# Forgetting attention: scores of two heads as 64-row products on the two halves of the array, for two query blocks in a row

## The chip, the cores and the metric

The kernel runs on one core of a Trainium2 chip. The time is the device time of one execution in microseconds; the figure for a kernel is the median of its runs. One further execution is recorded by the hardware profiler, and the rows shown in this document come from it. In the rows, PE is the matrix engine (TensorE) with its 128 x 128 array, PEld its weight loads, DVE the vector engine, ACT the scalar engine, POOL the GpSimd engine and SP the engine that mostly issues DMAs.

## The reference

A decoder of two layers over 512 positions of width 1024, in fp32. Layer 0 is a dilated windowed attention with a gated convolution network, layer 1 a forgetting attention with the same kind of network. The change lies in layer 1's attention. It has 16 heads of width 64; keys and values are made once from the residual stream, and so is a forget gate per head, whose cumulated logarithm `c` is added to the scores:

```python
for i in range(T // BLK):                      # blocks of 128 queries
    q0, q1 = i * BLK, (i + 1) * BLK
    s = einsum('bqhd,bkhd->bhqk', q[:, q0:q1], k[:, :q1]) * scale
    s = s + (c_t[:, :, q0:q1, None] - c_t[:, :, None, :q1])
    p = softmax(where(causal, s, NEG))
    outs.append(einsum('bhqk,bkhd->bqhd', p, v[:, :q1]))
```

Query block i sees the keys 0 to 128(i+1) - 1, so its scores are 128 by 128(i+1) for each head.

## The kernel before

**Number format.** Most products are made from fp32 values split in two parts, a high part rounded to the fast format fp32r and a low part, the remainder. A product then needs three terms: high times high, high times low, low times high (`mm3`, lines 263 to 266). Transposes and the product of probabilities and values are plain fp32.

**Work per head pair and unit.** Heads go in pairs, j = 0 to 7; head `2j + hh` has the 64 features `64hh` to `64hh + 63` of a 128-row chunk. A unit is (j, i), one pair and one query block, 32 in all, in order of j and then i. Scores are computed with the queries as weights (128 queries) and the keys as the moving operand, over `nn = max(128(i+1), 256)` columns.

**Stacked operands.** With heads of 64 features a score product would use only 64 of the array's 128 rows. The kernel stacks the two parts of an operand over the rows. For a key head, `keys` (line 1392) puts the high part in the 64 rows where the projection left it and the low part in the other 64 rows. For queries, `q_high` and `q_low` (lines 1505 and 1514) do the same for version 0 of a tile; two DMAs of 256 KB each, line 1523 and line 1524, copy it with its row halves exchanged into version 1. One product of 128 rows with version 0 then gives high times high plus low times low, and one with version 1 gives high times low plus low times high: `f_scores` (line 1583) makes two products per head, four per unit. For i < 2 the scores of both heads share a PSUM bank, for i >= 2 each head has a bank of its own. The DMAs are issued by SP, those of pair 0 by POOL.

**Order.** Every engine takes its instructions in the order in which the program writes them. The loop over n (line 1672) writes, for unit n: its scores (PE); the normalisation of unit n-1 (`f_norm`, DVE); the softmax of unit n (`f_exp`: on DVE, line 1604, the scaled score plus bias and its running extreme, on ACT, line 1606, the exponential with its sum); the bias of unit n+1 (`f_bias`, POOL); at i = 1 the low part of the next pair's queries; a quarter of a query projection for a later pair, six products of 512 columns (`q_part`, PE); the transposes of unit n-2's probabilities (`f_transpose`, PE, and ACT's copy at line 1630); and at i = 2 the products with the values for the four units of the pair before (`f_pv`, PE), whose 64-column halves serve one head each. At i = 0 follows the cast of the next pair's queries (`q_high`, ACT). In between, the weights for the output projection are loaded by SP (line 49), cast by ACT (line 57) and split by DVE (line 69). When no queries are left to project, from the seventh pair on, products of the output projection (`po`, tile `acc`) take their place.

**Buffers.** The eight PSUM banks are one pool; a new tile takes the bank that was released first in program order. Keys, queries, weights and outputs of the attention come from a pool of 16 tiles of 8 KB per partition (`t8`), biases, probabilities and raw weights from one of 10 tiles of 4 KB (`t4`).

Layer 0 has a related score product (lines 1111 and 1113): plain fp32, 64 rows, two heads on the two halves of the rows, not stacked. The profile shows each of its fp32 products as two passes.

Of the kernel before, what the change touches and what calls it, by code (L numbers as in the profile page):

```python
# [9 lines left out]
F32 = mybir.dt.float32  # L10
F32R = mybir.dt.float32r
BF16 = mybir.dt.bfloat16
AF = mybir.ActivationFunctionType
ALU = mybir.AluOpType

D = 1024
T = 512
# [86 lines left out]
def trunk_kernel(ctx, tc, x, norm_gains, w_qkv_a, w_o_a, w_q_b, w_o_b, kv_norm, w_kvf, b_f,  # L104
                 w_up, conv_w, conv_b, w_down, rope, out):
    nc = tc.nc
    act, dve, pool, pe, sp = nc.scalar, nc.vector, nc.gpsimd, nc.tensor, nc.sync
# [8 lines left out]
    def t8(shape, dt=F32, name="t8"):  # L116
        return p8.tile(shape, dt, tag="t8", name=name)

    def t4(shape, dt=F32, name="t4"):
        return p4.tile(shape, dt, tag="t4", name=name)  # L120
# [4 lines left out]
    def bank(shape, name="bank"):  # L125
        return psp.tile(shape, F32, tag="ps", name=name)

    def small(n, name):
        return sml.tile([128, n], F32, tag=name, name=name)
# [232 lines left out]
    def feat_mm(w, xT, o, s):  # L362
        wh, wl = (t.rearrange("p (k c) -> p k c", k=8) for t in w)
        for kc in range(KD):
            bh, bl = xs(xT, kc, s)
            mm3(o[:, s], wh[:, kc, :], wl[:, kc, :], bh, bl, kc == 0, kc == KD - 1)
# [1017 lines left out]

    kst = {}

    def halves(hh):

        own = slice(64 * hh, 64 * hh + 64)
        return own, slice(64 - 64 * hh, 128 - 64 * hh)  # L1390

    def keys(c):
        o = bank([128, T], name="k_ps")
        feat_mm(W.get(), bd2.xT, o, ALL)
        if c % 2 == 0:
            kst[c // 2] = t8([128, 4, T], F32R, name=f"kst{c // 2}")
        ts = [kst[(2 * c + hh) // 4][:, (2 * c + hh) % 4, :] for hh in range(2)]
        for hh in range(2):
            own, _ = halves(hh)
            act.copy(ts[hh][own], o[own])  # L1400
        for hh in range(2):
            own, other = halves(hh)
            dve.tensor_tensor(ts[hh][other], o[own], ts[hh][own].bitcast(F32), ALU.subtract)

    c8 = t2([16, T], name="c8")

# [78 lines left out]
    def load_ck(j):  # L1485
        t = t4([128, 2, T], name="ck")
        s = cd[2 * j:2 * j + 2, :]
        sp.dma_start(t, bass.AP(tensor=s.tensor, offset=s.offset, ap=[[0, 128], [T, 2], [1, T]]))
        cks[j] = t

    qT = {}
    qps = {}

    def q_part(j, i):

        if j >= 8:
            return
        if i == 0:
            qps[j] = (bank([128, T], name="q_ps"), [t.rearrange("p (k c) -> p k c", k=8) for t in W.get()])
        o, (wh, wl) = qps[j]  # L1500
        for kc in (2 * i, 2 * i + 1):
            bh, bl = xs(xTq, kc, ALL)
            mm3(o, wh[:, kc, :], wl[:, kc, :], bh, bl, kc == 0, kc == KD - 1)

    def q_high(j):
        if j >= 8:
            return
        o = qps[j][0]
        qT[j] = t = t8([128, 2, 2, T], F32R, name="qst")
        for hh in range(2):  # L1510
            own, _ = halves(hh)
            act.copy(t[own, 0, hh], o[own])

    def q_low(j):
        if j >= 8:
            return
        o, t = qps.pop(j)[0], qT[j]
        for hh in range(2):
            own, other = halves(hh)
            dve.tensor_tensor(t[other, 0, hh], o[own], t[own, 0, hh].bitcast(F32), ALU.subtract)  # L1520

        queue = sp if j else pool
        queue.dma_start(t[0:64, 1].bitcast(F32), t[64:128, 0].bitcast(F32))
        queue.dma_start(t[64:128, 1].bitcast(F32), t[0:64, 0].bitcast(F32))

    cd = tc.dram_tile([16, T], F32, name="cd")

# [45 lines left out]
    def f_bias(j, i):  # L1573
        n = (i + 1) * 128
        bias = t4([128, 2, T], name="bias")
        for hh in range(2):
            hd = 2 * j + hh
            pool.tensor_scalar(bias[:, hh, :n], cks[j][:, hh, :n], -1.0, cq[:, i, hd:hd + 1], ALU.mult, ALU.add)
        pool.affine_select(bias[:, :, n - 128:n], bias[:, :, n - 128:n], pattern=[[0, 2], [-1, 128]],
                           compare_op=ALU.is_ge, fill=NEG, base=0, channel_multiplier=1)  # L1580
        bia[j, i] = bias

    def f_scores(j, i):
        n = (i + 1) * 128
        nn = max(n, 256)
        if i < 2:
            o = bank([128, 2, 256], name="s_ps")
            s = [o[:, hh] for hh in range(2)]
        else:
            s = [bank([128, T], name="s_ps") for _ in range(2)]  # L1590
        for hh in range(2):
            hd = 2 * j + hh
            k = kst[hd // 4][:, hd % 4, :nn]
            for m in range(2):
                pe.matmul(s[hh][:, :nn], qT[j][:, m, hh, i * 128:(i + 1) * 128], k, start=m == 0, stop=m == 1)
        return s

    def f_exp(j, i, s):
        n = (i + 1) * 128
        bias = bia.pop((j, i))  # L1600
        p = t4([128, 2, T], name="prob")
        nm, ls = small(2, "nm"), small(2, "ls")
        for hh in range(2):
            dve.tensor_tensor_reduce(p[:, hh, :n], s[hh][:, :n], bias[:, hh, :n], -0.125, BIG, ALU.add, ALU.min,
                                     nm[:, hh:hh + 1])
            act.activation(p[:, hh, :n], p[:, hh, :n], AF.Exp, bias=nm[:, hh:hh + 1], scale=-1.0,
                           accum_out=ls[:, hh:hh + 1])
        prob[j, i] = (p, ls)

    def f_norm(j, i):  # L1610
        n = (i + 1) * 128
        p, ls = prob[j, i]
        rl = small(2, "rl")
        dve.reciprocal(rl, ls)
        for hh in range(2):
            dve.tensor_scalar(p[:, hh, :n], p[:, hh, :n], rl[:, hh:hh + 1], None, ALU.mult)
# [3 lines left out]
    def f_transpose(j, i):  # L1620
        p, _ = prob.pop((j, i))
        for hh in range(2):
            if i >= 2 or hh == 0:
                o = bank([128, 4, 128], name="pT_ps")
                t = t2([128, 4, 128], name="pT")
            k0 = (i + 1) * hh if i < 2 else 0
            for k in range(i + 1):
                pe.transpose(o[:, k0 + k, :], p[:, hh, k * 128:(k + 1) * 128], ident)
            if i >= 2 or hh == 1:
                act.copy(t[:, :k0 + i + 1], o[:, :k0 + i + 1])  # L1630
            pT[j, i, hh] = t[:, k0:k0 + i + 1]
# [4 lines left out]
    def f_pv(j, i):  # L1636
        if i == 0:
            ops[j] = bank([128, T], name="o_ps")
        o = ops[j]
        for k in range(i + 1):  # L1640
            for hh in range(2):
                hd = 2 * j + hh
                pe.matmul(o[64 * hh:64 * hh + 64, i * 128:(i + 1) * 128],
                          Vt[hd // 8][:, k, (hd % 8) * 64:(hd % 8) * 64 + 64], pT[j, i, hh][:, k, :],
                          start=k == 0, stop=k == i)
        del pT[j, i, 0], pT[j, i, 1]
# [8 lines left out]
    def f_out_low(j):  # L1655
        o, t = ops.pop(j), OTb[j // 2]
        dve.tensor_tensor(t[:, 1, j % 2, :], o, t[:, 0, j % 2, :].bitcast(F32), ALU.subtract)
# [14 lines left out]
    for n in range(N + 3):  # L1672
        live = n < N
        if live:
            j, i = units[n]
            if i == 0 and j + 1 < 8:
                load_ck(j + 1)
            s = f_scores(j, i)
        if 1 <= n <= N:
            f_norm(*units[n - 1])  # L1680
        if live:
            f_exp(j, i, s)
            if n + 1 < N:
                f_bias(*units[n + 1])
            if i == 1:
                q_low(j + 1)
                if 2 <= j < 6:
                    W.minus()
                    W.low_added()
            if i == 2 and j < 2 or (j, i) >= (6, 2):  # L1690
                W.low()
            if i == 3 and j:
                f_out_low(j - 1)
            q_part(j + 1 + (i > 0), (i + 3) % 4)
            if (j, i) in ((7, 1), (7, 2)):
                next(down1)
        if 2 <= n < N + 2:
            f_transpose(*units[n - 2])
        if n >= N + 3 - len(fill):
            po.both(*fill[n - N - 3 + len(fill)])  # L1700

        if n % 4 == 2 or n == N:
            while pv_next < n - 2:
                ju, iu = units[pv_next]
                pv_next += 1
                f_pv(ju, iu)
                if iu == 3:
                    f_out_high(ju)
        if live and i == 0:
            q_high(j + 1)  # L1710
        if live and (i == (j < 2) if j < 6 else (j, i) >= (6, 1) and W.n_split < wo + 4):
            W.high()
# [53 lines left out]
```

## Time and profile before

| | |
|---|---|
| median of three runs | 1113.82 us (1113.72 to 1114.44) |
| span of the profiled execution, first to last instruction | 1111.3 us |
| PE busy | 1101.0 us, 99% of the span |
| PE weight loads busy | 958.5 us, 86% |
| DVE busy | 888.2 us, 80% |
| ACT busy | 671.9 us, 60% |
| POOL busy | 216.7 us, 20% |
| keys, gates and values | about 540 to 613 us of the span |
| queries and attention of layer 1 | about 613 to 723 us of the span |
| HBM read and written | 166.08 MB and 39.63 MB |

Times in rows are microseconds from the span's start. A timeline row gives the start, the duration, the engine, the line, the operation, output and inputs, the shapes (rows x columns of the array in use, then output) and how many instructions stand in the row; brackets give idle time of the engine before it and what ended it. In a row of groups, after the bar, stand the busy time, the mean nanoseconds of one, and the idle time before. Matmuls are pipelined and their ends are modelled, so they overlap in the rows; what one costs is read from one start to the next.

### The profile page before, as it was taken

How to read it: one execution, taken by the hardware profiler on the slowest of the kernel's cores; microseconds unless marked ns; L12 is line 12 of the kernel's file. 1: busy time of each engine (PE TensorE's matmuls, PEld its weight loads, DVE VectorE, ACT ScalarE, POOL GpSimd, SP SyncE). 2: the span in 40 equal slices, each digit the busy share in tenths (PEclk: the TensorE clock that was granted, in tenths of full speed). 3: DMA queues.
4: the chain of work that ended last, by engine and by line, in shares of the span. 5: the costliest groups of instructions: out<-in, count | busy, mean ns of one | idle time of the engine just before them, and what ended most of it. 6: DMA issues, size and time to landing. Idle time of an engine off the chain costs nothing.

```text
span 1111.3 us, 18057 instructions
## 1 busy us (share of the span) xinstructions
PE 1101.0 (99%) x6546; PEld 958.5 (86%) x6546; DVE 888.2 (80%) x1500; ACT 671.9 (60%) x1104; POOL 216.7 (20%) x315
## 2 busy tenths in 40 slices
PE   9999999999999999999999999999999999999997
PEld 6988889899999988888878888889999999988886
DVE  6587788888788689997698777868887788779994
ACT  5454565656666747576462588756656666747572
POOL 2832001311111211000001545500411111211000
PEclk9999999999999999999999999999999999999999
DMA  9499864477887979793447667594378878988862
GB/s 326 171 343 412 319 181 135 87 182 188 212 193 185 247 259 324 280 328 107 133 152 263 212 158 173 187 284 120 83 178 208 195 186 189 241 261 312 318 246 76
DMA packets 185523, 240.46 MB, mean 216 GB/s; under 512 B 11929, under 2 KB 131721, under 8 KB 185434
## 3 DMA queue, kind: packets, MB, share of 16 engines
q1 hardware_dynamic: 170330, 186.61, 51.4%
q0 software_dynamic: 15104, 52.70, 20.8%
q8 instruction: 51, 0.84, 0.3%
q14 instruction: 38, 0.31, 0.1%
HBM read 166.08 MB, written 39.63 MB: 185 GB/s over the span
## 4 chain that ended last, share of the span: by engine, by line
PE 93%; issue 2%; DVE 2%; POOL 1%; DMA 1%; ACT 0%; DVEq 0%; SPq 0%; POOLq 0%
PE up L264 13%; PE up L266 13%; PE up L265 13%; PE acc L264 8%; PE acc L266 8%; PE acc L265 8%; PE qk_ps L264 2%; PE qk_ps L265 2%; PE qk_ps L266 2%; PE v_ps L264 2%; PE v_ps L266 2%; PE v_ps L265 2%; PE first L264 1%; PE first L266 1%; PE first L265 1%
## 5 line engine op out<-in xcount | busy, mean ns | idle before, releaser
L264 PE MATMUL acc<-w 128*128 128x512 f32 (+1 forms) x311 | 120.6, 388 | 0.3 <-DVE mix L326 0.3
L266 PE MATMUL acc<-w 128*128 128x512 f32 (+1 forms) x311 | 120.4, 387 | 0.0
L69 DVE TENSOR_TENSOR w<-wraw,w 128x1024 fp32r<-128x1024 f32 x74 | 97.5, 1333 | 26.0 <-ACT w L57 25.5
L57 ACT CAST w<-wraw 128x1024 fp32r<-128x1024 f32 x94 | 96.7, 1049 | 23.9 <-DMA wraw<-in_w_up_dram 7.4
L265 PE MATMUL acc<-w 128*128 128x512 f32 (+1 forms) x267 | 103.2, 387 | 0.0
L266 PE MATMUL up<-xsh,w 128*128 128x256 f32 x352 | 99.7, 283 | 0.0
L264 PE MATMUL up<-xsh,w 128*128 128x256 f32 x352 | 99.6, 283 | 0.0
L265 PE MATMUL up<-xsl,w 128*128 128x256 f32 x352 | 99.6, 283 | 0.0
L614 ACT ACTIVATE bb<-up,conv 128x512 f32<-128x512 f32 x80 | 59.6, 776 | 58.7 <-DVE up L1001 47.9
L265 PE MATMUL up<-xcl,w 128*128 128x512 f32 (+1 forms) x276 | 93.5, 339 | 0.0
L265 PE MATMUL up<-xbl,w 128*128 128x512 f32 (+1 forms) x276 | 93.5, 339 | 0.0
L264 PE MATMUL up<-xch,w 128*128 128x512 f32 (+1 forms) x276 | 93.5, 339 | 0.0
L264 PE MATMUL up<-xbh,w 128*128 128x512 f32 (+1 forms) x276 | 93.5, 339 | 0.0
L266 PE MATMUL up<-xbh,w 128*128 128x512 f32 (+1 forms) x276 | 93.4, 338 | 0.0
L266 PE MATMUL up<-xch,w 128*128 128x512 f32 (+1 forms) x276 | 93.4, 338 | 0.0
L264 PEld LDWEIGHTS acc<-w 128*128 128x128 f32 x311 | 58.4, 188 | 12.4 <-DVE mix L326 0.7
L266 PEld LDWEIGHTS acc<-w 128*128 128x128 f32 x311 | 58.4, 188 | 11.9
L266 PEld LDWEIGHTS up<-xsh,w 128*128 128x128 f32 x352 | 67.6, 192 | 0.2 <-DMA w<-wsum 0.2
L265 PEld LDWEIGHTS up<-xsl,w 128*128 128x128 f32 x352 | 67.6, 192 | 0.0
L264 PEld LDWEIGHTS up<-xsh,w 128*128 128x128 f32 x352 | 67.6, 192 | 0.0
L615 DVE SCALAR_TENSOR_TENSOR bb<-up,conv,bb 128x511 f32<-128x511 f32 x80 | 59.5, 744 | 6.8 <-ACT bb L614 6.8
L617 DVE SCALAR_TENSOR_TENSOR bb<-up,conv,bb 128x510 f32<-128x510 f32 x80 | 59.9, 749 | 2.8
(315 smaller groups left out, 3152.6 us busy)
## 6 DMA issues: line engine op xcount, KB each, us to landing
wraw<-in_w_up_dram SPq DMA_DIRECT2D x88, 512.0 KB, 5.6
w<-wraw POOLq DMA_DIRECT2D x32, 512.0 KB, 6.6
dT<-dsums SPq DMA_DIRECT2D x28, 512.0 KB, 7.5
w<-wsum POOLq DMA_DIRECT2D x24, 512.0 KB, 5.6
dsums<-in_w_down_dram SPq DMA_DIRECT2D x22, 512.0 KB, 7.8
dsums<-in_w_down_dram SPq DMA_DIRECT2D x44, 256.0 KB, 6.8
hD<-hc POOLq DMA_DIRECT2D x44, 256.0 KB, 7.2
dact<-hD SPq DMA_DIRECT2D x44, 256.0 KB, 5.5
```

What stands on the lines that cost most here:

```text
L57: self.nc.scalar.copy(pair[:, 0], raw)
L69: self.nc.vector.tensor_tensor(pair[:, 1], raw, pair[:, 0].bitcast(F32), ALU.subtract)
L264: pe.matmul(o, ah, bh, start=first, stop=False, skip_group_check=shared)
L265: pe.matmul(o, ah, bl, start=False, stop=False, skip_group_check=shared)
L266: pe.matmul(o, al, bh, start=False, stop=last, skip_group_check=shared)
L614: act.activation(bb[:, s, :], ps, AF.Identity, bias=cp[:, 3, ch:ch + 1], scale=cp[:, 2, ch:ch + 1])
L615: dve.scalar_tensor_tensor(bb[:, s, 1:], ps[:, :T - 1], cp[:, 1, ch:ch + 1], bb[:, s, 1:], ALU.mult, ALU.add)
L617: dve.scalar_tensor_tensor(bb[:, s, 2:], ps[:, :T - 2], cp[:, 0, ch:ch + 1], bb[:, s, 2:], ALU.mult, ALU.add)
```

## The change

- Keys and queries are not stacked any more. A key chunk is one tile with a high part and a low part, each of 128 rows, so two heads lie in the two row halves; one ACT cast and one DVE subtraction of 128 rows replace two of each of 64 rows. The same holds for queries, whose tile halves, and whose DMAs go.
- A score is made of three 64-row products, high times high, high times low, low times high, accumulated in one bank. Head 0 uses the first 64 rows of the array and head 1 the last 64; their products alternate in the program.
- Scores are written for two units in a row, at i = 0 for (0, 1) and at i = 2 for (2, 3), before the rest of the iteration. Each head has banks of its own: for i < 2 one bank per head holds both units, for i >= 2 each unit and head has a bank, four at once.

```diff
     def keys(c):
         o = bank([128, T], name="k_ps")
         feat_mm(W.get(), bd2.xT, o, ALL)
         if c % 2 == 0:
-            kst[c // 2] = t8([128, 4, T], F32R, name=f"kst{c // 2}")
-        ts = [kst[(2 * c + hh) // 4][:, (2 * c + hh) % 4, :] for hh in range(2)]
-        for hh in range(2):
-            own, _ = halves(hh)
-            act.copy(ts[hh][own], o[own])
-        for hh in range(2):
-            own, other = halves(hh)
-            dve.tensor_tensor(ts[hh][other], o[own], ts[hh][own].bitcast(F32), ALU.subtract)
+            kst[c // 2] = t8([128, 2, 2, T], F32R, name=f"kst{c // 2}")
+        k = kst[c // 2][:, c % 2]
+        act.copy(k[:, 0], o)
+        dve.tensor_tensor(k[:, 1], o, k[:, 0].bitcast(F32), ALU.subtract)
...
     def q_high(j):
-        o = qps[j][0]
-        qT[j] = t = t8([128, 2, 2, T], F32R, name="qst")
-        for hh in range(2):
-            own, _ = halves(hh)
-            act.copy(t[own, 0, hh], o[own])
+        qT[j] = t8([128, 2, T], F32R, name="qst")
+        act.copy(qT[j][:, 0], qps[j][0])
...
     def q_low(j):
         o, t = qps.pop(j)[0], qT[j]
-        for hh in range(2):
-            own, other = halves(hh)
-            dve.tensor_tensor(t[other, 0, hh], o[own], t[own, 0, hh].bitcast(F32), ALU.subtract)
-
-        queue = sp if j else pool
-        queue.dma_start(t[0:64, 1].bitcast(F32), t[64:128, 0].bitcast(F32))
-        queue.dma_start(t[64:128, 1].bitcast(F32), t[0:64, 0].bitcast(F32))
+        dve.tensor_tensor(t[:, 1], o, t[:, 0].bitcast(F32), ALU.subtract)
...
+    sc = {}
+
+    def f_scores(j, blocks):
+        wide = blocks[0] >= 2
+        if not wide:
+            both = [bank([128, 2, 256], name="s_ps") for _ in range(2)]
+        k = kst[j // 2][:, j % 2]
+        for i in blocks:
+            nn = max(256, (i + 1) * 128)
+            sc[j, i] = [bank([128, T], name="s_ps") for _ in range(2)] if wide else [o[:, i] for o in both]
+            for qp, kp in ((0, 0), (0, 1), (1, 0)):
+                for hh in range(2):
+                    own = slice(64 * hh, 64 * hh + 64)
+                    pe.matmul(sc[j, i][hh][:, :nn], qT[j][own, qp, i * 128:(i + 1) * 128], k[own, kp, :nn],
+                              start=qp + kp == 0, stop=qp == 1)
...
             if i == 0 and j + 1 < 8:
                 load_ck(j + 1)
-            s = f_scores(j, i)
+            if i % 2 == 0:
+                f_scores(j, (i, i + 1))
         if 1 <= n <= N:
             f_norm(*units[n - 1])
         if live:
-            f_exp(j, i, s)
+            f_exp(j, i)
```

`f_exp` takes its scores from `sc` in place of an argument and is otherwise unchanged.

More of the change, by code (lines that the diff above doesn't have):

```diff
@@ L1385, in trunk_kernel @@
     kst = {}
-    def halves(hh):
-        own = slice(64 * hh, 64 * hh + 64)
-        return own, slice(64 - 64 * hh, 128 - 64 * hh)
     def keys(c):
@@ L1581, in f_bias, with f_exp @@
         bia[j, i] = bias
-    def f_scores(j, i):
-        n = (i + 1) * 128
[L1585 to L1599, printed above, removed]
+    sc = {}
[12 more added lines that the diff above has]
+                              start=qp + kp == 0, stop=qp == 1)
+    def f_exp(j, i):
+        n = (i + 1) * 128
+        s = sc.pop((j, i))
         bias = bia.pop((j, i))
```

## The prediction

> **What bounds the kernel now.** First the page: the span, the busy shares and the chain that ended last.
>
> ```profile
> span 1111.3 us, 18057 instructions
> ...
> PE 1101.0 (99%) x6546; PEld 958.5 (86%) x6546; DVE 888.2 (80%) x1500; ACT 671.9 (60%) x1104; POOL 216.7 (20%) x315
> ...
> PE 93%; issue 2%; DVE 2%; POOL 1%; DMA 1%; ACT 0%; DVEq 0%; SPq 0%; POOLq 0%
> ```
>
> TensorE ends nearly everything. Next the windows of the two stages that the change touches, keys with gates and values, then queries with attention. Columns: length, then busy time of PE, PEld, DVE, ACT, POOL.
>
> ```profile
> 540.00:613.00 73.00, 73.00 (x324) 58.94 (x323) 56.60 (x73) 31.70 (x43) 5.33 (x10) 1.00 0.56 189
> 613.00:723.00 110.00, 108.06 (x787) 92.36 (x785) 83.98 (x259) 85.90 (x213) 58.12 (x104) 1.00 0.63 179
> ```
>
> In the keys' stage PE is never idle; in attention it lacks 1.94 of 110 us. The clock is full in both (1.00). So I count in TensorE time, and other engines only where PE is seen waiting. A busy PE overlaps its matmuls, so costs are read from start to start. The timeline of one unit, with 256 columns, and the page by score tile:
>
> ```profile
> 658.11 0.60 PE L1628 MATMUL pT_ps<-ident,prob 128*128 128x128 f32 x4
> 658.46 0.72 PE L1595 MATMUL s_ps<-kst,qst 128*128 128x256 f32 x4
> 659.02 0.40 PE L264 MATMUL q_ps<-xqh,w 128*128 128x512 f32 x1
> 659.25 0.39 PE L265 MATMUL q_ps<-xql,w 128*128 128x512 f32 x1
> ```
>
> ```profile
> L1595 PE MATMUL s_ps<-kst,qst x128: 277/338/504, 623.2 to 720.3; 128*128 128x256 f32 x64, 128*128 128x384 f32 x32, 128*128 128x512 f32 x32
> L1113 PE MATMUL s_ps<-qkT x64: 272/272/373, 89.8 to 127.0; 64*128 64x128 f32 x64
> ```
>
> A pass of 128 fp32 columns lasts 0.272 us as recorded, so four transposes in 0.60 start (0.60-0.27)/3 = 0.109 apart. From 658.11 to 659.02 are 0.91; less 4 x 0.109, four score products take 0.474, 0.118 each. A 512-column product takes 0.23 (659.02 to 659.25), one of 384, between them, 0.175. Per head pair: 8 x 0.118 + 4 x 0.175 + 4 x 0.23 = 2.56 us; eight pairs 20.5 us. That is all the score work.
>
> **The change, part by part.**
>
> *Products.* Four of 128 rows become six of 64 rows, two heads at a time. If the halves run together, a unit costs three products' time instead of four: 2.56/4 = 0.64 saved per pair, 5.1 us in all. This kernel has no fp32r product on 64 rows. Its nearest rows are layer A's fp32 scores, two heads on two row halves:
>
> ```profile
> 61.26 0.39 PE L266 MATMUL qk_ps<-w,xpl 128*128 128x512 f32 x1
> 61.57 2.10 PE L1111 MATMUL s_ps<-qkT 64*128 64x256 f32 x16
> ```
>
> Sixteen passes of 256 columns; at the transposes' rate one is 0.218, sixteen in file 3.5 us. They took 2.10, of which some 0.1 is the first weight load (below) and 0.27 the last one's end: 1.73, eight pairs of 0.216. Two halves overlap fully there. I take full overlap for fp32r; the other end is none, six products in file, +2.56/2 x 8 = +10.2 us.
>
> The Trainium skill ("TensorE: Matmul & The Clock Gate", Measured speedup vs the span model) gives 3.07x measured for four row tiles where four would be ideal. An estimate from that page, the same loss for two, 1.53x, would make a pair cost 1.3 products and leave 0.5 of the 5.1 saved, so that the sum would be +3.7 instead of -0.9. The row above disagrees: 3.5/1.73 is 2.0x, but in fp32, whose column takes twice as long as fp32r's; no run here shows two tiles at the full rate.
>
> *Changing the array's shape.* The array was used whole for scores, transposes and projections, split only for the probabilities-times-values product (64 columns). Layer A shows what a 64-row block costs at its edges:
>
> ```profile
> 89.32 0.60 PE L1086 MATMUL qkT_ps<-ident,qk 128*128 128x128 f32 x4
> 89.85 1.56 PE L1113 MATMUL s_ps<-qkT 64*128 64x128 f32 x16
> 91.34 0.50 PE L264 MATMUL qk_ps<-w,xph 128*128 128x512 f32 x1
> 91.68 0.39 PE L265 MATMUL qk_ps<-w,xph 128*128 128x512 f32 x1
> ```
>
> In: the transposes end streaming at 89.32 + 4 x 0.109 = 89.76, the block starts at 89.85, 0.09 later, and its first product lasts 0.373 instead of 0.272 (minimum and maximum above), 0.10 more, because its weights start loading only then: 0.19. Out: the block's last pass starts at 91.41 - 0.27 = 91.14 and ends streaming near 91.25; the next product, with its weight load, starts at 91.34 (0.09) and takes 0.34 to the next start instead of 0.23 (0.10): 0.19-0.20. Together 0.39. The present scores pay none, as the sum above (0.91) shows. A check by the split that exists:
>
> ```profile
> 666.06 0.38 PE L1628 MATMUL pT_ps<-ident,prob 128*128 128x128 f32 x2
> 666.37 2.40 PE L1643 MATMUL o_ps<-pT,Vt 128*64 128x128 f32 x40
> 668.71 1.20 PE L1595 MATMUL s_ps<-kst,qst 128*128 128x512 f32 x4
> 669.75 0.39 PE L264 MATMUL q_ps<-xqh,w 128*128 128x512 f32 x1
> ```
>
> From 666.06 to 669.75 are 3.69; content 2 x 0.109 + 20 pairs x 0.109 + 4 x 0.23 = 3.32: 0.37 in and out. With scores of two units in a row there are two blocks per pair, at i = 0 (after transposes) and i = 2 (after transposes too): 16 blocks x 0.39 = +6.2 us. Ends: 0.37 each, 5.9; or 0.18, 2.9, if the weight loads were hidden.
>
> *Order.* Unit i+1's scores pass the query part, the transposes and the values product on PE's queue. At i = 2 those get about 1.1 us later (3 x 0.23 + 0.39). Who waits is ACT's copy of the transposes, and DVE's first step gets both heads after three pairs, not one head after two products:
>
> ```profile
> 666.66 0.56 DVE L1604 CUSTOM_DVE_ANT_0 prob<-s_ps,bias 128x384 f32<-128x384 f32 x1
> ...
> 668.48 0.35 ACT L1630 COPY pT<-pT_ps 128x256 f32<-128x256 f32 x1
> ```
>
> The copy runs 2.2 us after its transposes (666.06 + 0.22), and DVE reads unit 2's scores 2.8 us after they start (663.89, next): both have the slack. At i = 0 the delay (3 x 0.118 + 0.39, 0.7 us) reaches the copies, and ACT gets back 0.58 of it at once from the query cast below. Cost zero; if the cover were gone, up to 0.5 us per pair, 4 us.
>
> *Banks.* Units 2 and 3 want four PSUM banks at once; the last two are those that units 0 and 1 leave when DVE has read unit 1.
>
> ```profile
> 663.89 0.94 PE L1595 MATMUL s_ps<-kst,qst 128*128 128x384 f32 x4
> 663.91 0.42 DVE L1604 CUSTOM_DVE_ANT_0 prob<-s_ps,bias 128x256 f32<-128x256 f32 x1
> ```
>
> DVE is done at 664.33; unit 3's first product would want its bank at 663.89 + 0.19 + 3 x 0.175 = 664.6. Zero, margin 0.3 us.
>
> *Casts and DMAs.* Half-row pairs become one instruction of 128 rows:
>
> ```profile
> L1512 ACT CAST qst<-q_ps 64x512 fp32r<-64x512 f32 x16 | 9.3, 582 | 7.5 <-PE q_ps L266 7.3
> L1400 ACT CAST kst<-k_ps 64x512 fp32r<-64x512 f32 x16 | 9.3, 582 | 18.6 <-PE k_ps L266 18.4
> L1653 ACT CAST OTb<-o_ps 128x512 fp32r<-128x512 f32 x7 | 4.1, 592 | 0.3
> ```
>
> ```profile
> L1520 DVE TENSOR_TENSOR qst<-q_ps,qst 64x512 fp32r<-64x512 f32 x16 | 11.0, 689 | 5.9 <-ACT qst L1512 5.5
> L1657 DVE TENSOR_TENSOR OTb<-o_ps,OTb 128x512 fp32r<-128x512 f32 x7 | 4.8, 683 | 0.0
> ```
>
> 128 rows cost what 64 do, so ACT and DVE each lose half, 0.58 and 0.69 us per pair and as much per key chunk. The keys' half is hidden, PE being full there: nothing. The sixteen DMAs (SP, two on POOL) go, and with them two waits of PE. The first is direct:
>
> ```profile
> 631.91 0.36 PE L1595 MATMUL s_ps<-kst,qst 128*128 128x256 f32 x1
> 632.61 0.59 PE L1595 MATMUL s_ps<-kst,qst 128*128 128x256 f32 x3 [0.34 <-DMA qst<-qst]
> ```
>
> 0.70 where 0.118 is due: -0.6 us. The second goes through SP's queue, where weight loads stand behind the query's copies:
>
> ```profile
> 703.29 1.22 SPq L1524 DMA_DIRECT2D qst<-qst  x1
> 704.61 1.70 SPq L49 DMA_DIRECT2D wraw<-in_w_o_b_dram  x3
> ```
>
> ```profile
> 708.70 1.05 ACT L57 CAST w<-wraw 128x1024 fp32r<-128x1024 f32 x1 [1.83 <-DMA wraw<-in_w_o_b_dram]
> 712.49 1.07 PE L1628 MATMUL pT_ps<-ident,prob 128*128 128x128 f32 x8 [1.58 <-DVE prob L1616]
> ```
>
> The late load holds ACT 1.83, the exponential behind it, the normalisation, and PE 1.58. Without the copies SP issues it earlier, and the cast starts some 1.8 sooner; PE then arrives about when the row is ready. Late next is DVE's weight split ahead of that normalisation, so I take -1.4; ends 0 and -1.6.
>
> *Sum*: -5.1 + 6.2 - 0.6 - 1.4 = -0.9 us on 1111.3. The median, 1113.82, lies 2.5 above the span, which I leave as it is: 1112.9.
>
> **The rivals.**
>
> *Serial halves (slower).* The fp32r pair runs in file. For: no fp32r row on 64 rows. Against: layer A's eight pairs. +10.2 + 6.2 - 0.6 - 1.6 = +14.2: 1128. It decides from a pair longer than about 1.2 products.
>
> *Partly packed, or a new wait (slower).* Three pairs in place of four products gain nothing once a pair costs 4/3 of a product. Just short of it, at 1.3, the stream is 20.0 us against 20.5: -0.5 + 6.2 - 2.0 = +3.7, 1117.5; with full overlap a new wait of 0.6 us per head pair gives as much. For: the thin bank margin, the moved ACT copies. Against: 2.0x in layer A. The Trainium skill's measured packing, above, speaks for it.
>
> *Cheap edges (faster).* Weight loads slip under the drain: 2.9 for edges, -5.1 + 2.9 - 2.0 = -4.2: 1109.6. For: fp32r streams twice as fast. Against: both edges in layer A.
>
> **How the numbers follow.** The forecast, changed by less than 0.2% (2.2 us, about what a measurement of this kernel tells from none): 0.45. Serial 0.16, partly packed 0.17, faster 0.22. The range takes in the cheap edges and the partly packed case, not the serial one: 1109 to 1121. Of the likeliest alone: 1111.6 to 1116. Faster 0.22, same 0.45, slower 0.33.
>
> **What would show it.** The timeline: six-product blocks of 64 rows, 12 per two units; block i = 0 from its first start to the next projection near 0.2 + 6 x 0.118 + 0.1 = 1.0 us if paired, 1.7 if serial. First projection after a block 0.34 to the next. No wait of a score on a DMA; the wait at the seventh pair's last transposes small; the o-weights' loads earlier. DVE some 11 us less busy in total (16 x 0.69), ACT 9 (16 x 0.58). Wrong if pairs run in file, or if PE waits for DVE or ACT at the banks or the copies.

## The result, and the profile after

The changed kernel takes 1112.28 us (median of 14 runs, 1111.76 to 1114.07). The kernel before, run beside it, takes 1114.47 (14 runs, 1112.89 to 1117.24). The ratio is 0.998, interval 0.9973 to 0.9987: about 2.2 us faster. The forecast of 1112.9 lies 0.6 us from it, but the change itself, -2.2, is more than twice the -0.9 of the forecast's sum.

The span of the profiled execution fell less, from 1111.3 to 1110.8 us. The page of the kernel after, its span, its busy times and its chain of work:

```profile
span 1110.8 us, 18056 instructions
...
PE 1101.9 (99%) x6610; PEld 952.9 (86%) x6610; DVE 876.8 (79%) x1484; ACT 660.6 (59%) x1088; POOL 214.9 (19%) x313
...
PE 94%; DVE 2%; DMA 1%; issue 1%; ACT 1%; POOL 1%; DVEq 0%; SPq 0%; POOLq 0%; ACTq 0%
```

TensorE still carries 94% of the chain. DVE has 11.4 us less to do and ACT 11.3. That alone buys no time that the runs can tell: an experiment below keeps it, brings the copies back, and has no gain.

The windows of the two stages after (length, then busy time of PE, PEld, DVE, ACT and POOL, then the granted clock, the DMA share and GB/s):

```profile
540.00:613.00 73.00, 73.00 (x325) 59.09 (x324) 50.57 (x65) 26.64 (x35) 5.33 (x10) 1.00 0.60 197
613.00:723.00 110.00, 109.30 (x853) 87.54 (x852) 79.16 (x251) 80.25 (x206) 56.42 (x102) 1.00 0.46 135
```

In the keys' stage DVE and ACT lose 6.0 and 5.1 us, and PE is as full as it was: the keys' half is hidden. In attention PE lacks 0.70 us of 110, where it lacked 1.94, and the DMA share falls from 0.63 to 0.46, since the sixteen exchange copies are gone.

Two blocks of scores, from the timeline of the kernel after (start, duration, engine, line, operation): a pair's first two units (256 columns), and its last two (384 and 512 columns).

```profile
671.34 0.60 PE L1612 MATMUL pT_ps<-ident,prob 128*128 128x128 f32 x4
671.87 0.98 PE L1578 MATMUL s_ps<-kst,qst 64*128 64x256 f32 x12
672.77 0.50 PE L264 MATMUL q_ps<-xqh,w 128*128 128x512 f32 x1
673.11 0.40 PE L265 MATMUL q_ps<-xql,w 128*128 128x512 f32 x1
...
677.27 1.49 PE L1578 MATMUL s_ps<-kst,qst 64*128 64x384 f32 x12
678.69 0.50 PE L264 MATMUL q_ps<-xqh,w 128*128 128x512 f32 x1
679.02 0.40 PE L265 MATMUL q_ps<-xql,w 128*128 128x512 f32 x1
```

The block starts at 671.87 and the next projection at 672.77: 0.90 us, where 1.0 was forecast for paired halves and 1.7 for serial ones. Twelve products cost six times 0.118. The projection behind the block takes 0.34 to the next start, as forecast. Edges: the last transpose started at 671.34 + 3 x 0.109 = 671.67, and the second projection at 673.11, 1.44 later (1.448 in the finer starts of the trace). Content is one transpose, six pairs and one projection, 0.109 + 6 x 0.118 + 0.231 = 1.05. The edges are the rest, 0.40, where the sum had 0.39.

By tile, the cast and the subtraction of the query after, over 128 rows (shortest, median, longest in ns; first and last start):

```profile
L1500 ACT CAST qst<-q_ps x8: 589/603/605, 614.2 to 701.6; 128x512 fp32r<-128x512 f32 x8
L1506 DVE TENSOR_TENSOR qst<-q_ps,qst x8: 680/691/693, 614.8 to 702.2; 128x512 fp32r<-128x512 f32 x8
```

Twice the rows cost 603 and 691 ns instead of 582 and 689, so half of this work is gone, as forecast.

The second wait of the forecast, the one that goes through SP's queue, in the timelines of SP, ACT and PE after:

```profile
699.81 5.70 SPq L49 DMA_DIRECT2D wraw<-in_w_o_b_dram  x3
```

```profile
706.88 1.10 ACT L57 CAST w<-wraw 128x1024 fp32r<-128x1024 f32 x1
```

```profile
711.51 1.17 PE L1612 MATMUL pT_ps<-ident,prob 128*128 128x128 f32 x8 [0.39 <-DVE prob L1600]
```

SP issues the first of the late weights' loads at 699.81 instead of 704.61. ACT's cast runs at 706.88, with no wait, instead of 708.70 after 1.83 us of it. PE's idle before the seventh pair's last transposes falls from 1.58 to 0.39. A small new wait follows, 0.30 us at 716.28, for ACT's copy of transposes.

One thing was forecast at nothing and is not quite nothing. The second pair's late block, and the last pair's with DVE's reads and PE's weight loads beside it, from the timeline after:

```profile
637.97 1.81 PE L1578 MATMUL s_ps<-kst,qst 64*128 64x384 f32 x12
639.71 0.50 PE L264 MATMUL q_ps<-xqh,w 128*128 128x512 f32 x1
...
713.99 1.99 PE L1578 MATMUL s_ps<-kst,qst 64*128 64x384 f32 x12
```

```profile
714.21 0.41 DVE L1588 CUSTOM_DVE_ANT_0 prob<-s_ps,bias 128x256 f32<-128x256 f32 x1
714.55 0.41 DVE L1588 CUSTOM_DVE_ANT_0 prob<-s_ps,bias 128x256 f32<-128x256 f32 x1
714.68 0.18 PEld L1578 LDWEIGHTS s_ps<-kst,qst 64*128 64x128 f32 x1 [0.23 <-DVE nm L1588]
715.03 0.19 PEld L1578 LDWEIGHTS s_ps<-kst,qst 64*128 64x128 f32 x2 [0.16 <-DVE nm L1588]
```

The block takes 1.49 in the pair shown above, so these two are 0.32 and 0.50 longer. In the last pair the products of the fourth unit wait for DVE to read the second unit out of its bank: the reads end at 714.62 and 714.96, and the weights of each head load 0.06 and 0.07 later. Two of eight late blocks are longer in this execution. In a second traced execution of the same kernel (y_again below) the last pair's is 0.50 longer again, the second pair's only 0.07.

### The profile page after: what moved, and what is told of

Its sections match the earlier page's. It is cut to its first block, busy times and chain, and to the rows that moved or that the text cites. A ratio compares the mean times of both kernels' runs of the same rounds, so it can differ in the third digit from the quotient of the medians.

```text
span 1110.8 us, 18056 instructions
## 1 busy us (share of the span) xinstructions
PE 1101.9 (99%) x6610; PEld 952.9 (86%) x6610; DVE 876.8 (79%) x1484; ACT 660.6 (59%) x1088; POOL 214.9 (19%) x313
## 4 chain that ended last, share of the span: by engine, by line
PE 94%; DVE 2%; DMA 1%; issue 1%; ACT 1%; POOL 1%; DVEq 0%; SPq 0%; POOLq 0%; ACTq 0%
PE up L266 12%; PE up L265 12%; PE up L264 12%; PE acc L264 8%; PE acc L265 8%; PE acc L266 8%; PE v_ps L264 2%; PE v_ps L266 2%; PE v_ps L265 2%; PE qk_ps L265 2%; PE qk_ps L264 2%; PE qk_ps L266 2%; PE q_ps L264 1%; PE first L266 1%; PE first L264 1%; PE first L265 1%
```

## Experiments

The theory: halves overlap fully, each change of the array's shape costs about 0.2 us, and these two nearly cancel; the gain is that of the vanished exchange copies. Rivals: the gain comes from the tiles themselves, from the order of the units, or from the lighter ACT and DVE. Differences below are between medians: to the kernel before run on the same chip (1114.37 to 1114.47), to the changed kernel's 1112.28, or 1112.35 where y_again ran beside. A ratio is always to the kernel before.

**The kernel before without its exchange copies (x_nodma).** ACT and DVE write the exchanged query themselves.

```diff
-            own, _ = halves(hh)
+            own, other = halves(hh)
             act.copy(t[own, 0, hh], o[own])
+            act.copy(t[other, 1, hh], o[own])
...
+            dve.tensor_tensor(t[own, 1, hh], o[own], t[own, 0, hh].bitcast(F32), ALU.subtract)
-        queue = sp if j else pool
-        queue.dma_start(t[0:64, 1].bitcast(F32), t[64:128, 0].bitcast(F32))
-        queue.dma_start(t[64:128, 1].bitcast(F32), t[0:64, 0].bitcast(F32))
```

> The kernel before, with the exchanged version of the queries written by ACT and DVE themselves (two more casts of 0.58 us and two more subtractions of 0.69 us per pair) and without the sixteen DMAs. Theory of the ledger: both waits of PE behind those DMAs go, 0.6 at the second pair and up to 1.7 at the seventh's transposes, since SP's weight load no longer stands behind the copies; the extra ACT and DVE work is covered in pairs 0 to 5. Expected -1 to -2 us against the kernel before. Rival, the DMAs cost more than the one profile shows: -3 or more, and then most of the change's gain is theirs. Second rival, the extra ACT and DVE work gives a later chain: 0 or slower.

Measured: 1128.41 us (1128.24 to 1128.59), ratio 1.013, interval 1.0117 to 1.0144; 14 us slower, so the expectation fails and its second rival holds. Its window over attention, and PE's two longest waits in it (us in total, times, longest):

```profile
613.00:730.00 117.00, 106.44 (x715) 86.89 (x714) 88.45 (x251) 87.80 (x211) 56.79 (x100) 0.99 0.44 133
```

```profile
PE o_ps L1641 <- ACT pT L1628: 6.4, 5, 2.4
PE pT_ps L1626 <- DVE prob L1614: 1.5, 3, 0.6
```

PE now lacks 10.6 of 117 us, mostly waiting for ACT's copies of the transposes. The edit puts two more casts (2 x 0.58) and two more subtractions (2 x 0.69) into each pair, and PE comes to wait for ACT. So it does not isolate the copies. What it does show is that ACT and DVE, about 76 to 78% busy in this stage before, are close to becoming the bound.

**The order alone, with the scores of before (x_pairs).**

```diff
-            s = f_scores(j, i)
+            if i % 2 == 0:
+                sc[j, i], sc[j, i + 1] = f_scores(j, i), f_scores(j, i + 1)
+            s = sc.pop((j, i))
```

> The kernel before, with scores written for two units in a row and nothing else changed: products stay at 128 rows, stacked, with the DMAs. Theory of the ledger: order and banks alone cost and gain nothing, within 0.5 us of the kernel before. Rival, the gain is that of the order (odd units' scores ready earlier): -2 us. Second rival, the order costs bank waits: +0.5 to +1 us.

Measured: 1117.55 us (1115.79 to 1118.52), ratio 1.003, interval 1.0019 to 1.0042; 3.2 slower, so the expectation fails. PE's three longest waits in attention:

```profile
PE pT_ps L1628 <- DVE prob L1616: 1.7, 1, 1.7
PE s_ps L1595 <- DMA qst<-qst: 1.7, 3, 1.3
PE o_ps L1643 <- DVE qst L1520: 0.8, 1, 0.8
```

Scores wait for the copies 1.7 us in all instead of 0.3: in the last pair SP issues the first of them at 703.44 instead of 702.60, and the scores stand 1.27 us. The values product waits 0.8 for DVE's subtraction of the query, which it did not before. Why DVE and the copies are later was not traced. In the changed kernel no copy stands before the scores, and such a wait is not seen. The order by itself is no source of the gain.

**The changed kernel with the sixteen copies back, into a half that nobody reads (y_dma).**

```diff
-        qT[j] = t8([128, 2, T], F32R, name="qst")
+        spare[j] = t8([128, 2, 2, T], F32R, name="qst")
+        qT[j] = spare[j][:, 0]
...
+        t = spare.pop(j)
+        queue = sp if j else pool
+        queue.dma_start(t[0:64, 1].bitcast(F32), t[64:128, 0].bitcast(F32))
+        queue.dma_start(t[64:128, 1].bitcast(F32), t[0:64, 0].bitcast(F32))
```

> The changed kernel, with the sixteen DMAs of the kernel before put back after each query cast, of the same size and in the same queues, onto a part of the tile that nothing reads; no product waits for them. Theory of the ledger: SP's weight load of the seventh pair is late again and with it the transposes' wait, so about +1.2 us over the changed kernel, about -1 against the kernel before. Rival, the load's time does not matter: same as the changed kernel, -2.

Measured: 1114.15 us (1113.44 to 1115.63), ratio 1.0002, interval 0.9992 to 1.0011. The gain of 2.2 is gone but for 0.2, which the interval can't tell from nothing. Against the changed kernel 1.9 came where about 1.2 was expected. The timelines of SP and PE:

```profile
703.10 1.15 SPq L1512 DMA_DIRECT2D qst<-qst  x1
704.35 1.70 SPq L49 DMA_DIRECT2D wraw<-in_w_o_b_dram  x3
```

```profile
712.14 1.17 PE L1618 MATMUL pT_ps<-ident,prob 128*128 128x128 f32 x8 [1.37 <-DVE prob L1606]
```

Nobody waits for these copies; their data is not used. Still the loads behind them in SP's queue go out at 704.35 again, and PE waits 1.37 us again. The tiles, the order and the lighter ACT and DVE are all still there, so within the interval, about 1 us to either side, none of these rivals makes the gain. That it is the load's place in the queue that costs is what the next run tries.

**One load moved ahead in the kernel before (x_load_first).** Everything else stays: 128-row scores, single units, exchange copies.

```diff
             if i == 1:
+                if j == 6:
+                    W.load(W.n_split + 1 + W.ahead_dma)
                 q_low(j + 1)
```

> The kernel before, with one thing moved: at the seventh pair's second iteration SP issues the next weight load of the output projection ahead of the query's two exchange DMAs instead of behind them. Theory of the ledger: the cast on ACT no longer waits for it (1.83 us) and PE's wait of 1.7 us before the seventh pair's last transposes shrinks by more than one: -1.0 to -1.4 us against the kernel before. Rival, the next work in that chain is as late: 0.

Measured: 1112.28 us (1111.49 to 1115.4), ratio 0.9985, interval 0.9975 to 0.9994: 2.2 faster, the same time as the whole change, and more than the 1.0 to 1.4 that was expected. Its SP, ACT and PE timelines:

```profile
698.59 0.33 SPq L49 DMA_DIRECT2D wraw<-in_w_o_b_dram  x1
701.96 0.47 SPq L1523 DMA_DIRECT2D qst<-qst  x1
```

```profile
706.28 1.05 ACT L57 CAST w<-wraw 128x1024 fp32r<-128x1024 f32 x1
```

```profile
710.72 1.10 PE L1628 MATMUL pT_ps<-ident,prob 128*128 128x128 f32 x8 [0.40 <-DVE prob L1616]
```

The load goes out ahead of the query's copies, ACT's cast does not wait, and PE's idle at the seventh pair is 0.40, as in the changed kernel. The copies themselves are still there. So it is the place in the queue that costs, and one issue in another place gives, in the old kernel, what the rewrite gives.

**The changed kernel, one unit at a time (y_single).** Each pair now has four blocks of 64 rows instead of two.

```diff
-            if i % 2 == 0:
-                f_scores(j, (i, i + 1))
+            f_scores(j, (i,))
```

> The changed kernel with scores of one unit at a time, at the start of each iteration: four 64-row blocks per pair instead of two. Theory of the ledger, edges of 0.39 us per block: unit 1's block adds 0.39 per pair; unit 3's stands right behind the values product, whose way out it shares, and adds 0.20. Together 0.59 x 8 = +4.7 us over the changed kernel, about +2.5 against the kernel before. Rival, edges are cheap or hidden behind other waits: +1 or less.

Measured: 1115.89 us (1115.36 to 1116.87), ratio 1.0017, interval 1.0008 to 1.0025; 3.6 slower than the changed kernel. One block in its timeline:

```profile
673.47 0.60 PE L1612 MATMUL pT_ps<-ident,prob 128*128 128x128 f32 x4
674.00 0.62 PE L1578 MATMUL s_ps<-kst,qst 64*128 64x256 f32 x6
674.55 0.50 PE L264 MATMUL q_ps<-xqh,w 128*128 128x512 f32 x1
674.89 0.40 PE L265 MATMUL q_ps<-xql,w 128*128 128x512 f32 x1
```

From 673.47 to 674.89 are 1.42 us. Content is 4 x 0.109 + 3 x 0.118 + 0.231 = 1.02, so the edges are 0.40 again: they belong to the block, not to its length. The block at i = 3 follows the values product:

```profile
668.44 0.38 PE L1612 MATMUL pT_ps<-ident,prob 128*128 128x128 f32 x2
668.75 2.40 PE L1627 MATMUL o_ps<-pT,Vt 128*64 128x128 f32 x40
671.09 0.96 PE L1578 MATMUL s_ps<-kst,qst 64*128 64x512 f32 x6
671.98 0.50 PE L264 MATMUL q_ps<-xqh,w 128*128 128x512 f32 x1
672.31 0.40 PE L265 MATMUL q_ps<-xql,w 128*128 128x512 f32 x1
```

From 668.44 to 672.31 are 3.87 us. Content is 2 x 0.109 + 20 x 0.109 + 3 x 0.230 + 0.231 = 3.32, so the edges are 0.55, where the values product alone pays 0.37. This block adds about 0.2, as expected, and the edges of both some 4.7 in all. Only 3.6 came: the late blocks' waits for banks, 0.3 and 0.5, are not there in this form, and PE's idle in the stage falls from 0.70 to 0.38.

**The changed kernel again, and with the values product put next to the scores (y_again, z_pv).** If an edge costs 0.2, a split block that directly follows another split block should save one. In pairs 0 to 5 the values product is moved to just ahead of the next pair's first scores.

```diff
+            if i == 0:
+                values_of(n - 4)
             if i % 2 == 0:
...
-            if i == 3 and j:
-                f_out_low(j - 1)
+            if i == 1 and j >= 2:
+                f_out_low(j - 2)
+            if (j, i) == (7, 3):
+                f_out_low(6)
...
-        if n % 4 == 2 or n == N:
+        if n >= N - 2 and n % 2 == 0:
+            values_of(n - 2)
```

(`values_of` is the loop that stood at the end of the iteration, as a function.)

> The changed kernel itself, as the mark for the runs beside it: about -2.2 us against the kernel before, within 0.7.

> The changed kernel, with the values product of pair j-1 moved from the end of iteration (j, 2) to the start of iteration (j+1, 0), right before the 64-row scores, for pairs 0 to 5; the low part of its output follows two iterations later. Both use a split array, so one way out to the whole array and one way in fall together. Theory of the ledger: 0.19 us saved per pair, six pairs, -1.2 us against the changed kernel. Rival, a change from a column split to a row split costs both edges as before: 0. Second rival, the later values product or the longer hold of the transposed probabilities makes a new wait: slower than the changed kernel.

Measured: 1112.35 us for the changed kernel (1111.62 to 1113.03; ratio 0.9983, interval 0.9975 to 0.9992) and 1111.22 for the moved product (1110.64 to 1112.3; ratio 0.9971, interval 0.9962 to 0.998). That is 1.1 less (1.2 was expected), though the two intervals overlap a little. In its timeline:

```profile
667.80 0.60 PE L1612 MATMUL pT_ps<-ident,prob 128*128 128x128 f32 x4
668.32 2.40 PE L1627 MATMUL o_ps<-pT,Vt 128*64 128x128 f32 x40
670.66 0.98 PE L1578 MATMUL s_ps<-kst,qst 64*128 64x256 f32 x12
671.57 0.50 PE L264 MATMUL q_ps<-xqh,w 128*128 128x512 f32 x1
671.90 0.40 PE L265 MATMUL q_ps<-xql,w 128*128 128x512 f32 x1
```

From 667.80 to 671.90 are 4.10 us. Content is 4 x 0.109 + 20 x 0.109 + 6 x 0.118 + 0.231 = 3.56. The three edges are 0.54 together, where two separate blocks would pay 0.37 + 0.40 = 0.77. That is 0.23 a pair, and six pairs give 1.4. PE's waits in the stage grow from 0.70 to 1.03 us, which takes 0.3 of it back.

**The same, with pair 5's product left in place, and repeated (z_pv5, z_pv_again).** In the kernel just shown PE waits for DVE at 702.56 (0.42 us) and for ACT's copy at 711.26 (0.61 us). Does leaving one product where it was take the first away?

```diff
-            if i == 0:
+            if i == 0 and j < 7:
                 values_of(n - 4)
...
```

(Against the kernel just shown; the low part of that pair's output and the last calls of `values_of` move with it.)

> The changed kernel with the values product moved before the 64-row scores for pairs 0 to 4 only; that of pair 5 stays where the changed kernel has it, where PE, without query projections to fill it, otherwise waits 0.6 us for DVE. Expected 0.4 us below the version with six pairs moved, about 1.5 below the changed kernel, 1110.8. Rival: the waits of pairs 6 and 7 only change places, the same as with six.

> The version with the values products of pairs 0 to 5 moved, as the mark for the runs beside it: about -3.2 us against the kernel before, within 0.8.

Measured: 1111.79 us (1111.32 to 1112.27; ratio 0.9974, interval 0.9963 to 0.9985) and 1111.36 (1111.18 to 1111.88; ratio 0.997, interval 0.9958 to 0.9981). The first has five products moved, the second is the kernel with six again. With five, PE waits 0.57 us for DVE at 710.25 and 0.29 for ACT at 715.02. The waits change places and one shared edge less is saved: no time is won, the 0.4 us expected did not come, and the rival holds. The version with six products moved stays the fastest found, 0.003 below the kernel before in both of its measurements.

**Both heads on the same half of the rows (y_same_half).** No overlap is then possible.

```diff
-                    own = slice(64 * hh, 64 * hh + 64)
+                    own = slice(0, 64)
```

> The changed kernel, with the second head's products taken from the first head's 64 rows, so that all six products of a unit use the same half of the array and follow each other; this leaves out the second head's scores, and its output is that of wrong scores. Theory of the ledger: without overlap the stream grows by three products per unit, 15.4 us in all, to 30.9; so +14 to +15.4 us over the changed kernel, less what the few waits give back. Rival, the two halves overlap only in the records' starts: a good deal less.

Measured: 1126.39 us (1125.97 to 1128.39), ratio 1.0112, interval 1.0098 to 1.0126; 14.0 above the changed kernel. Its timeline and its window over attention:

```profile
670.43 2.71 PE L1578 MATMUL s_ps<-kst,qst 64*128 64x384 f32 x12
```

```profile
613.00:740.00 127.00, 127.00 (x879) 104.28 (x879) 81.92 (x257) 82.33 (x208) 56.29 (x103) 1.00 0.41 122
```

The late block takes 2.71 instead of 1.49: six products of 384 and six of 512 columns in file. From full overlap to none is 5.1 + 10.2 = 15.3 by the forecast's sum. 14.0 came. PE now waits for nothing (127.00 of 127.00 busy) and so covers 0.70 us of idle that it had, and the last pair's late block takes 2.72, so its 0.5 for the bank is covered too. The two halves of the changed kernel do overlap in full.

**Written head by head (y_by_head).** The three products of one head stand in the program before those of the other.

```diff
-            for qp, kp in ((0, 0), (0, 1), (1, 0)):
-                for hh in range(2):
+            for hh in range(2):
+                for qp, kp in ((0, 0), (0, 1), (1, 0)):
```

> The changed kernel, with the three products of the first head written before the three of the second instead of alternating. Theory: the halves have their own order, as layer 0's scores show, which are written head by head and start in pairs; so the same as the changed kernel, within 0.5 us. Rival, products start in program order: the first two of head 0 run alone, and a unit takes up to six products' time, up to +15 us.

Measured: 1112.89 us (1112.13 to 1114.01), ratio 0.9989, interval 0.998 to 0.9998; 0.5 above the changed kernel, within the intervals. In its timeline:

```profile
671.61 0.98 PE L1578 MATMUL s_ps<-kst,qst 64*128 64x256 f32 x12
672.53 0.50 PE L264 MATMUL q_ps<-xqh,w 128*128 128x512 f32 x1
```

The block is as short as before (671.61 to 672.53). The products start in pairs, 10 ns apart instead of 3 to 4. The records do not name the head; but two products of one head stand in file, as the run before shows, so the two of a pair belong to the two heads. The halves do not need to be interleaved in the program, at least with three products a head.

## Why the prediction was right, step by step

*Products* (-5.1, full overlap) held. Pairs start about every 0.118, 0.176 and 0.231 us, as single 128-row products did, and without the overlap the kernel is 14.0 us slower. The forecast's evidence was thinner than it said. Its other block of 64 rows in layer 0 (89.85 to 91.34) has sixteen passes of 128 columns in 1.49 us, 1.30 without the edges inside it; full overlap would be 8 x 0.109 = 0.87 and none 16 x 0.109 = 1.74. That block overlapped in part only, and the forecast did not count this against itself. The Trainium skill's 3.07x for four tiles ("TensorE: Matmul & The Clock Gate", Measured speedup vs the span model) had given +3.7 by an estimate; this trace has 2.0x for two, so the loss that this page measured for four does not carry over to these two.

*Changing the array's shape* (+6.2) held: 0.40 a block against 0.39, a little less in two of the last blocks, which transposes follow (0.37 and 0.34); about +6.3 in all. The Trainium skill ("TensorEngine Tiling (Array Packing)", Key Properties) says that switching the mode drains the array but gives no price; here the price is about 0.2 us for each edge. By these two terms the tiles are worth +1.2, a loss, so the change would not have paid by them alone. No run shows this pair of terms by itself. The nearest is the changed kernel with the unread copies; by the terms it should end 0.6 above the kernel before (+1.2, and -0.6 for the first wait). By medians it ends level with it, with an interval that holds the 0.6. In its trace the stretch from the first query product to the last values product takes 133.78 us against 133.20, 0.6 longer.

*Order* (0) held for the changed kernel, but the reason given did not cover the copies. In the old form the same order costs 3.2 us, and the forecast's slack of 2.2 and 2.8 us at ACT and DVE says nothing of that. ACT's copies did cost something, too: the new wait of 0.30 for one of them.

*Banks* (0, margin 0.3) was a little too small. Two of eight late blocks are longer, by 0.3 and 0.5 us (0.07 and 0.5 in the second traced execution); in the last pair the rows above show the bank as the cause.

*Casts and DMAs* held in kind. The keys' half is hidden. The first wait is gone (-0.6 forecast; at that place scores follow the transposes at once). The second went from 1.58 to 0.39, so -1.2 where -1.4 was taken, and what is late next is DVE's normalisation, as named. DVE lost 11.4 us of work (forecast 11). ACT lost 11.3 where 9 was forecast; the casts of query and key make 9.1 of these, and the other 2 are not traced.

*Sum*: -0.9 forecast. The profiled pair shows -0.5 and the medians -2.2. In the profiles, from the first query product to the last values product attention takes 133.20 us before and 132.78 after, -0.4. The terms as measured are -5.1 and +6.3, +0.8 at the banks, +0.3 for the copy, -0.6 and -1.2 for the two waits: +0.5, so the ledger lacks 0.9 us of gain. Most of this lies in the values products, which the forecast left alone. Before, two of the seven whole blocks of forty took longer than the others. One of them, with a wait for ACT's copy, and the same one after:

```profile
702.12 2.85 PE L1643 MATMUL o_ps<-pT,Vt 128*64 128x128 f32 x40
703.88 0.85 PEld L1643 LDWEIGHTS o_ps<-pT,Vt 128*64 128x64 f32 x14 [0.26 <-ACT pT L1630]
```

```profile
703.66 2.40 PE L1627 MATMUL o_ps<-pT,Vt 128*64 128x128 f32 x40
```

That is 0.45 us, and the one at 653.05 (2.69) makes 0.29 more: together -0.7, a term that the forecast does not have. In the changed kernel every whole block takes 2.40. Which part of the change brought this was not traced. The remaining 0.2 is less than the 0.3 by which two traced executions of the changed kernel differ in this stretch.

The larger part of -2.2 lies between profile and median, and there the forecast's base was off. It saw the median 2.5 us above the profiled span and left that as it was. In the runs whose span was recorded, it is 1.7 to 1.9 us shorter than the time. So some 0.7 of the 2.5 belongs to the profiled execution, which was a quick one: of 66 recorded spans of the kernel before, 5 are 1111.3 or less, and the middle one is 1112.7. The changed kernel's profiled span, 1110.8, lies 0.2 above the middle one of its 14 runs. A quick execution of the one is thus compared with an ordinary one of the other. What an ordinary execution of the kernel before does longer, no trace shows. It seems to go with the copies: brought back, they shift the median by 1.9, where the traced stretch grows by 1.0, and the load moved ahead in the old kernel gives 2.2 in the median and 1.6 in the profiled span. That a late load costs some executions more than the profiled one would explain it, but it stays open.

So the mechanism was right, and the nearness of 1112.9 to 1112.28 is in part luck. The change came out more than twice as large as forecast, while the kernel before took 1114.47 beside it and not the 1113.82 that the forecast added to.

Of the rivals, serial halves and partly packed halves fall with the starts in pairs, and the new waits, 0.8 at the banks and 0.3 at the copy, stay far below 0.6 in every pair. Cheap edges came nearest in time (1109.6 against 1112.28) but not in kind: the edges cost the full 0.4, and what exceeded the forecast went away when the copies were brought back.

## What to carry to other kernels

Price every change of the array's shape, here 0.4 us for a way in and out, against what the split saves, and put split stages next to each other so that they share an edge. Before rewriting a stage for its copies, look in the DMA queue for what stands behind them: here one load issued earlier gave the same 2.2 us as the whole rewrite. An engine that is 75 to 80% busy in a chain of dependent steps may have little to give: here 1.2 us more work on ACT and 1.4 on DVE in each pair cost 14 us in all. And before adding a forecast to a median, see whether the profiled execution was an ordinary one: here it was 1.4 us quicker than the middle one.

## What the runs showed of the hardware that was not expected

The two row halves keep an order of their own, as far as starts and lengths tell. Written head by head, products start in pairs, 10 ns apart, so the second head's first one starts ahead of products that stand earlier in the program, and the block is as short as the interleaved one.

A split by columns followed by a split by rows (the values product, then the scores) costs three edges of 0.54 us in all instead of the four of 0.77.

A copy whose data nobody reads can still cost TensorE 1 us, by holding back the load that stands behind it in its queue.
